# Four transformer mixers, a hybrid block and PEER on one Trainium2 core: another tile order and modulation schedule in GLA, statistics inside the turning at layer ends, FoX values copied by ScalarE

## The chip, the cores and the metric

The kernel runs on one core of one Trainium2 chip. The metric is the device time of one execution in microseconds (us). TensorE (PE) multiplies, VectorE (DVE), ScalarE (ACT) and GpSimd (POOL) work on elements, and SyncE (SP) issues most of the transfers from HBM. Each engine runs its own instructions in the order in which they were written; semaphores join them.

## The reference, cut to what matters

All is float32, for one sequence of 256 tokens and width 1024.

```
cond = silu(c)
for i in range(4):
    mod = cond @ w_mod[i] + b_mod[i]
    shift, scale, gate = split(mod, 3)
    h = rms_norm(x, norm_pre_g[i]) * (1.0 + scale) + shift
    # i = 0, 3: gated linear attention; 1: spatial gating; 2: forgetting attention
    o = (gla_mixer, sgu_mixer, fox_mixer)[i % 3](h, ...)
    x = x + gate * rms_norm(o, norm_post_g[i])
x = x + hybrid_mixer(rms_norm(x, norm_mix), ...)
x = x + peer_ffn(rms_norm(x, norm_ffn), ...)
return rms_norm(x, final_norm)

def gla_mixer(h, ...):
    q, k, v, z, a_low = split(h @ w_in)
    log_a = log_sigmoid(a_low @ w_a2 + b_a) / 16
    # by chunks of 64 tokens: scores q k^T with decay, values, a running state
    o = rms_norm(o, g_head)
    return (o * silu(z)) @ w_out

def fox_mixer(h, ...):
    q, k, v, z, f_logit = split(h @ w_in)
    q, k = rms_norm(q, g_q), rms_norm(k, g_k)
    F = cumsum(log_sigmoid(f_logit + b_f))
    # causal softmax attention with F[q] - F[k] added to the scores
    return (o * silu(z)) @ w_out
```

## The kernel before, in words

**Stages.** After a start of some 37 us come the four mixers one behind the other: GLA (layer 0) to about 170 us, SGU (layer 1) to 292, FoX (layer 2) to 472, GLA again (layer 3) to 599. Then the hybrid block runs to about 925 and PEER to the end. The change touches the four mixers and the place where one layer's output becomes the next layer's input.

**Weights.** A weight tile is 512 KB in HBM (`wr`, 128x1024). SP loads it into one of `RAW = 4` buffers. `w_split` turns it into a high and a low part: ACT writes `wh` (L200), and DVE writes `wl = wr - wh` (L201). A product then takes three matmuls: L403 to L405 in `proj_fm` and L420 to L422 in `proj_tm`. The splits run `LEAD = 5` tiles ahead of the matmuls, in `HIGH = 6` buffers. `proj_fm` ("FM") gives columns by tokens, 24 matmuls of 256 columns for a tile. `proj_tm` ("TM") gives tokens by columns for the two blocks of 128 tokens (tb0 and tb1), matmuls of 512 columns. Projections write into `PJ = 3` PSUM buffers `pj`; other products go to `pm`.

**Ticks.** The functions that work beside the projections are generators. `tick()` is called after each weight tile and lets every listed generator write its next part. The order of the instructions is therefore fixed by how often a generator yields; there is no scheduler.

**Modulation.** For each layer SCALE, SHIFT and GATE are sums over 8 chunks of `w_mod`, 512 KB each. `m_step` does one chunk: DVE multiplies it and adds it to `macc` (L252 for the first of eight, L254 for the others), and SP is given the load of the chunk two further on, in 3 buffers. After the eighth, `m_cols` adds the rows up on PE (L266), copies them on ACT (`rows_copy`, L304), turns them to columns on PE (`rows_to_cols`, L313) and finishes them on DVE as `modc` (L271 to L276), with yields between. GLA layer 0 has 24 steps on its list: GATE of its own, then SCALE and SHIFT of the next layer. `out_proj` turns the GATE columns on PE (L478) and multiplies each output block by them (L484).

**GLA.** Its projections come in the order v (2 TM groups), k (4 FM tiles), q (4), z (8), then the output projection. DVE copies q out of PSUM (L628, `qk`); the scores are L652 and L654, the masks L656.

**Layer ends.** In the last group of `out_proj` all tiles of tb0 come before those of tb1. `late(tb)` makes the statistics of a token block (L355, L492 to L500, one power on POOL), adds to x (L505), norms (L361) and hands over to `make_h`: PE turns two halves of four 128x128 blocks (L367), ACT scales them, DVE writes `hH` and `hL` (L388, L389) in four pairs. The next layer's first projection takes tb0 for a whole tile group and then tb1. The table `FILL` sets when weight splits are written around this place.

**FoX.** q and k leave PSUM on ACT (L830, and squares L832); DVE sums the squares (L833, L840), ACT takes the root (L841, L842), DVE multiplies (L847), and PE turns the result (L790). v is copied by DVE (L861). The forget gate F itself is made elsewhere (L822 and on).

Of the kernel before, what the change touches and what calls it, by code (L numbers as in the profile page):

```python
# [8 lines left out]
F32 = mybir.dt.float32  # L9
F32R = mybir.dt.float32r  # L10
I32 = mybir.dt.int32
U32 = mybir.dt.uint32
AF = mybir.ActivationFunctionType
# [3 lines left out]
P = 128  # L17
# [8 lines left out]
RAW = 4  # L26
HIGH = 6
LEAD = 5
FILL = ((5, 6, 0, 0), (7, 8, 0, 0))
PJ = 3  # L30
RAW2 = 3
HIGH2 = 3
# [29 lines left out]
def _build(ctx, nc, tc, I, out, dbg):  # L62
# [32 lines left out]
    def add(gen, to=tasks):  # L95
        to.append(gen)
# [50 lines left out]
    def plan_fm(t, n, nk=KT):  # L147
        plan.extend((t[c], nk) for c in range(n))
# [4 lines left out]
    for l in range(4):  # L153
        if l in (0, 3):
            j = l // 3
            plan_tm(I["gla_v"][j], 2)
            plan_fm(I["gla_qk"][j], 8)
            plan_fm(I["gla_z"][j], 8)
            plan_tm(I["gla_out"][j], 2)
        elif l == 1:  # L160
            plan_tm(I["sgu_v"], 2)
            plan_fm(I["sgu_uz"], 16)
            plan_tm(I["sgu_out"], 2)
        else:
            plan_tm(I["fox_qkv"], 6)
            plan_fm(I["fox_z"], 8)
            plan_tm(I["fox_out"], 2)
# [38 lines left out]
    def w_fill(n):  # L206
        while nxt_s[0] < n:
            nxt_s[0] += 1
            w_split(nxt_s[0] - 1)
# [48 lines left out]
    def m_cols(l, part):  # L258
        acc = mods.pop((l, part, "acc"))
        mc = tiny.tile([P, 8], F32, tag=f"modc{part}", name="modc", bufs=2)  # L260
        mods[l, part] = mc
        for _ in range(2 if part == SHIFT else 4):
            yield
        p = pm()
        for g in range(4):
            mm(p[32 * g:32 * g + 32, 0:S], ones[:, 0:32], acc[:, g * S:(g + 1) * S], start=True, stop=True)  # L266
        yield
        R = rows_copy(p, 4)
        yield
        pcv = rows_to_cols(p, 4, R)  # L270
        tt(mc.rearrange("p (g t) -> p t g", t=2), pcv.rearrange("p t (g r) -> p t g r", r=32)[:, :, :, 0],  # L271
           col("b_mod", l * 24 + part * 8, 8).rearrange("p (g t) -> p t g", t=2), op=ALU.add)
        if part == SCALE:
            stt(mc, mc, 1.0, col("g_pre", l * 8, 8), op0=ALU.add, op1=ALU.mult)
        elif part == GATE:
            tt(mc, mc, col("g_post", l * 8, 8), op=ALU.mult)  # L276
# [53 lines left out]
    def advance():  # L330

        for g in list(pend):
            if next(g):
                pend.remove(g)
                turning.append(g)

    def settle():
        while pend:
            advance()
        while turning:  # L340
            for _ in turning.pop(0):
                pass
# [27 lines left out]
    def make_h(tb, r, A, B, hs):  # L370

        h, hH, hL = hs
        tsl = slice(tb * P, (tb + 1) * P)
        xn = scaled(tb, r)
        yield True
        ps = [turned(v) for v in xn]
        for m, p in enumerate(ps):
            k4 = slice(4 * m, 4 * m + 4)
            t = h[:, k4, tsl] if h is not None else work.tile([P, 4, P], F32, tag="tl", name="tl", bufs=2)
            for j in range(4):  # L380
                kt = 4 * m + j
                if B is None:
                    act(t[:, j], p[:, j], AF.Copy, scale=A[:, kt:kt + 1])
                else:
                    act(t[:, j], p[:, j], AF.Identity, scale=A[:, kt:kt + 1], bias=B[:, kt:kt + 1])
                if j % 2:
                    e = slice(kt - 1, kt + 1)
                    nc.vector.tensor_copy(hH[:, e, tsl], t[:, j - 1:j + 1])  # L388
                    tt(hL[:, e, tsl], t[:, j - 1:j + 1], hH[:, e, tsl].bitcast(F32), op=ALU.subtract)  # L389

    def proj_fm(n, H, L, consume, nk=KT, per_block=False):

# [19 lines left out]
    def proj_tm(n, H, L, consume, early=False, late=None):  # L412


        def part(p, w, c, tb):
            wh, wl = w
            tsl = slice(tb * P, (tb + 1) * P)
            for k in range(2):
                kt = c * 2 + k
                mm(p, H[:, kt, tsl], wh[:, k], start=(kt == 0), stop=False)  # L420
                mm(p, H[:, kt, tsl], wl[:, k], start=False, stop=False)  # L421
                mm(p, L[:, kt, tsl], wh[:, k], start=False, stop=(kt == KT - 1))  # L422

        for gi in range(n):
            if early and gi == 0 or late is not None and gi == n - 1:
                first = nxt_w[0]
                ws = []
                p = pj()
                for c in range(4):
                    ws.append(w_next(False))  # L430
                    part(p, ws[c], c, 0)
                    advance()
                    if FILL[0][c]:
                        w_fill(first + FILL[0][c])
                consume(gi, 0, p)
                settle()
                if late is not None:
                    pend.append(late(0))
                    advance()
                p = pj()  # L440
                for c in range(4):
                    part(p, ws[c], c, 1)
                    advance()
                    if FILL[1][c]:
                        w_fill(first + FILL[1][c])
                    tick()
                consume(gi, 1, p)
                if late is not None:
                    settle()
                    pend.append(late(1))  # L450
                    advance()
                continue
            ps = [pj() for _ in range(NTB)]
            for c in range(4):
                w = w_next()
                for tb in range(NTB):
                    part(ps[tb], w, c, tb)
                if c == 3:
                    for tb in range(NTB):
                        consume(gi, tb, ps[tb])  # L460
                tick()
# [59 lines left out]
        yield  # L521
        tt(dst, dst, t1, op=ALU.subtract)

    def gated(o, oH, oL, hH, hL, zt, ready, tanh=False):

        zs = {}

        def gate():
            last = None
            for b in range(KT):  # L530
                while b >= ready[0] or b not in zs:
                    yield
                tt(o[:, b], o[:, b], zs.pop(b), op=ALU.mult)
                act(oH[:, b], o[:, b], AF.Copy)
                if last is not None:
                    tt(oL[:, last], o[:, last], oH[:, last].bitcast(F32), op=ALU.subtract)
                last = b
                if b % 2:
                    yield
            tt(oL[:, last], o[:, last], oH[:, last].bitcast(F32), op=ALU.subtract)  # L540

        def c_z(b, p):
            z = zt[:, b]
            if tanh:
                act(z, p, AF.Tanh, scale=0.5)
                stt(z, z, 1.0, p, op0=ALU.add, op1=ALU.mult)
            else:
                act(z, p, AF.Silu)
            zs[b] = z

        add(gate())
        proj_fm(8, hH, hL, c_z, per_block=True)


    def gla(l, hs, lp, nA, nB, nF):
# [58 lines left out]
            have["decay"] = True  # L614

        add(decay())
        add(mod_steps([1] * (8 if l else 24)), later)

        def c_v(g, tb, p):
            if tb == 1:  # L620
# [79 lines left out]
                    yield  # L700

        proj_fm(4, hH, hL, c_k)
        add(mix(0))
        add(mix(1))
        assert have["decay"]
        proj_fm(4, hH, hL, c_q)
        oH = lp.tile([P, KT, S], F32R, tag="kk", name="oH")
        oL = lp.tile([P, KT, S], F32R, tag="qk", name="oL")
        gated(o, oH, oL, hH, hL, lp.tile([P, KT, S], F32, name="zt"), ready)
        drain()  # L710
        return out_proj(oH, oL, lp, ("ls1", "v"), l, nA, nB, nF)

# [91 lines left out]
    def fox(l, hs, lp, nA, nB, nF):  # L804
# [33 lines left out]
        def normed(half):  # L838
            sv = ss[:, half]
            ts(sv, sv, 1.0 / Dh, EPS, op0=ALU.mult, op1=ALU.add)  # L840
            act(sv, sv, AF.Ln)  # L841
            act(sv, sv, AF.Exp, scale=-0.5)  # L842
            yield
            yield
            for tb in range(NTB):
                vw = qk[:, tb, half * D:(half + 1) * D].rearrange("p (h d) -> p h d", d=Dh)
                tt(vw, vw, sv[:, tb, :, None].to_broadcast([P, 16, Dh]), op=ALU.mult)  # L847
                yield
            yield
            yield from transpose_blocks(qk[:, :, half * D:(half + 1) * D], qkT[:, 8 * half:8 * half + 8], 8,  # L850
                                        col("g_k" if half else "g_q"), done)

        add(mod_steps([1] * 24), later)
        add(forget())
        proj_tm(2, hH, hL, c_qk, early=True)
        add(normed(0))
# [1 line left out]
        add(normed(1))  # L858

        def c_v(g, tb, p):  # L860
            nc.vector.tensor_copy(v[:, tb, g * 512:(g + 1) * 512], p)  # L861

        SP = ((0, 0, P), (P, P, S))
        ready = [0]
# [795 lines left out]
```

## Time and profile before

| | |
|---|---|
| median of 3 runs | 1792.31 us (1790.88 to 1793.3) |
| the profiled execution | 1794.16 us |
| its span, first to last instruction | 1792.2 us |
| mean granted TensorE clock | 0.978 of full speed |
| PE busy | 1690.8 us |
| DVE busy | 1286.6 us |
| ACT busy | 970.5 us |

The span is 1.96 us shorter than the time of the same execution. The profiled execution is 1.85 us above the median. PE's busy time holds matmuls at either level of its clock, so a stretch in which PE is always busy can still be slow.

### The profile page before, as it was taken

What the parts mean: (1) busy time and instruction counts of PE and PEld (TensorE: products, weight loads), DVE (VectorE), ACT (ScalarE), POOL (GpSimd) and SP (SyncE); (2) the same over time, 40 slices, a digit from 0 to 9 for tenths busy, and PEclk for the clock granted to TensorE, in tenths of its full rate; (3) what the DMA queues carried; (4) which work ended last, traced back from release to release, by engine and by line L of the source; (5) the groups of instructions that cost most, each with busy time, mean ns of one, the idle gap of its engine ahead of it and who ended that gap; (6) DMA issues with size and microseconds to landing.
All of it is one profiled execution on the core that took longest, in us unless ns stands there. A gap on an engine that the chain in (4) does not pass through costs nothing.

```text
span 1792.2 us, 28529 instructions
## 1 busy us (share of the span) xinstructions
PE 1690.8 (94%) x10774; PEld 1492.5 (83%) x10774; DVE 1286.6 (72%) x2593; ACT 970.5 (54%) x1527; POOL 62.2 (3%) x102
## 2 busy tenths in 40 slices
PE   3979899999989999999999999999999999999997
PEld 2877786767789788888979999998999888888886
DVE  7878787877785856675576889997774466666665
ACT  3436446545644644435454446667995555555554
POOL 0000000000000000000000000000000000000000
PEclk9989999999989999999999999999999999999999
DMA  8765885862463566335654676664557677877775
GB/s 328 262 220 194 285 285 175 302 233 74 146 213 105 158 209 181 118 102 152 187 174 136 206 225 190 204 192 159 150 150 231 214 240 235 234 236 234 236 235 159
DMA packets 104188, 357.08 MB, mean 199 GB/s; under 512 B 12273, under 2 KB 13297, under 8 KB 103794
## 3 DMA queue, kind: packets, MB, share of 16 engines
q1 hardware_dynamic: 97200, 335.52, 59.6%
q0 software_dynamic: 5120, 16.78, 2.4%
q10 hardware_dynamic: 1730, 2.96, 0.5%
q8 instruction: 85, 1.39, 0.3%
q14 instruction: 53, 0.43, 0.1%
HBM read 337.38 MB, written 17.83 MB: 198 GB/s over the span
## 4 chain that ended last, share of the span: by engine, by line
PE 76%; DVE 11%; DMA 5%; ACT 4%; issue 3%; SPq 0%; POOL 0%; DVEq 0%; POOLq 0%; ACTq 0%
PE pm L1447 20%; PE pj L1424 6%; PE pj L1422 6%; PE pj L1423 6%; PE pj L420 5%; PE pj L422 4%; PE pj L421 4%; PE pj L403 4%; DMA wmod<-in_w_mod 4%; PE pj L404 4%; PE pj L405 4%; DVE wl L201 4%; PE pm L1329 3%; DVE macc L254 2%; ACT wh L200 1%
## 5 line engine op out<-in xcount | busy, mean ns | idle before, releaser
L201 DVE TENSOR_TENSOR wl<-wr,wh 128x1024 fp32r<-128x1024 f32 x504 | 614.7, 1224 | 306.0 <-ACT wh L200 305.5
L200 ACT ACTIVATE wh<-wr 128x1024 fp32r<-128x1024 f32 x504 | 528.1, 1055 | 217.9 <-PE pm L1447 54.8
L1422 PE MATMUL pj<-uH,wh 128*128 128x256 f32 x1024 | 293.7, 287 | 0.0
L1424 PE MATMUL pj<-uL,wh 128*128 128x256 f32 x1024 | 289.9, 283 | 0.0
L1423 PE MATMUL pj<-uH,wl 128*128 128x256 f32 x1024 | 289.8, 283 | 0.0
L403 PE MATMUL pj<-hH,wh 128*128 128x256 f32 x768 | 228.1, 297 | 1.6 <-DVE v L623 0.9
L404 PE MATMUL pj<-hH,wl 128*128 128x256 f32 x768 | 222.9, 290 | 0.6 <-DVE wl L201 0.4
L405 PE MATMUL pj<-hL,wh 128*128 128x256 f32 x768 | 222.2, 289 | 0.0
L1447 PE MATMUL pm<-wh 128*128 128x512 f32 x512 | 203.1, 397 | 4.1 <-ACT wh L321 4.1
L1447 PE MATMUL pm<-wl,wh 128*128 128x512 f32 x512 | 202.8, 396 | 0.0
L1447 PE MATMUL pm<-wh,wl 128*128 128x512 f32 x512 | 202.7, 396 | 0.0
L1422 PEld LDWEIGHTS pj<-uH,wh 128*128 128x128 f32 x1024 | 196.7, 192 | 0.0
L1423 PEld LDWEIGHTS pj<-uH,wl 128*128 128x128 f32 x1024 | 196.4, 192 | 0.1
L1424 PEld LDWEIGHTS pj<-uL,wh 128*128 128x128 f32 x1024 | 196.2, 192 | 0.0
L420 PE MATMUL pj<-wh,hH 128*128 128x512 f32 x352 | 146.5, 416 | 22.4 <-DVE hH L388 14.8
L403 PEld LDWEIGHTS pj<-hH,wh 128*128 128x128 f32 x768 | 152.7, 199 | 13.0 <-issue 7.9
L404 PEld LDWEIGHTS pj<-hH,wl 128*128 128x128 f32 x768 | 152.8, 199 | 1.4 <-DVE wl L201 1.3
L405 PEld LDWEIGHTS pj<-hL,wh 128*128 128x128 f32 x768 | 152.6, 199 | 0.0
L422 PE MATMUL pj<-wh,hL 128*128 128x512 f32 x352 | 142.2, 404 | 0.3 <-DVE hL L1527 0.3
L421 PE MATMUL pj<-wl,hH 128*128 128x512 f32 x352 | 141.7, 403 | 0.0
L254 DVE SCALAR_TENSOR_TENSOR macc<-wmod,sc,macc 128x1024 f32<-128x1024 f32 x76 | 97.3, 1281 | 33.3 <-DMA wmod<-in_w_mod 33.0
L1447 PEld LDWEIGHTS pm<-wh 128*128 128x128 f32 x512 | 96.5, 188 | 27.6 <-ACT wh L321 4.3
(337 smaller groups left out, 2679.1 us busy)
## 6 DMA issues: line engine op xcount, KB each, us to landing
wr<-in_down SPq DMA_DIRECT2D x128, 512.0 KB, 3.8
wr<-in_up SPq DMA_DIRECT2D x128, 512.0 KB, 4.3
wmod<-in_w_mod SPq DMA_DIRECT2D x88, 512.0 KB, 5.7
wr<-in_hyb_fm SPq DMA_DIRECT2D x40, 512.0 KB, 3.6
wr<-in_hyb_qkv SPq DMA_DIRECT2D x36, 512.0 KB, 4.3
spill<-st POOLq DMA_DIRECT2D x64, 256.0 KB, 3.8
a<-spill SPq DMA_DIRECT2D x64, 256.0 KB, 3.4
wr<-in_fox_qkv SPq DMA_DIRECT2D x24, 512.0 KB, 4.1
```

Of the source, the lines that this page charges most:

```text
L200: act(wh, w, AF.Copy)
L201: tt(wl, w, wh.bitcast(F32), op=ALU.subtract)
L403: mm(o, wh[:, kt, cs], H[:, kt], start=(kt == 0), stop=False)
L404: mm(o, wl[:, kt, cs], H[:, kt], start=False, stop=False)
L405: mm(o, wh[:, kt, cs], L[:, kt], start=False, stop=(kt == nk - 1))
L420: mm(p, H[:, kt, tsl], wh[:, k], start=(kt == 0), stop=False)
L421: mm(p, H[:, kt, tsl], wl[:, k], start=False, stop=False)
L422: mm(p, L[:, kt, tsl], wh[:, k], start=False, stop=(kt == KT - 1))
L1422: mm(o, wh[:, kt], uH[:, kt], start=(kt == 0), stop=False)
L1423: mm(o, wl[:, kt], uH[:, kt], start=False, stop=False)
L1424: mm(o, wh[:, kt], uL[:, kt], start=False, stop=(kt == KT - 1))
L1447: mm(acc[tb][n], lw[:, m, tsl], ru[:, 0, HALF[n]], start=(i == 0 and lw is wh and ru is uh), stop=(i == P - 1 and lw is wl))
```

## The change: what it does

Five parts. (A) In both GLA layers two of the eight z tiles run between k and q (`ZFIRST = 2`), so that nine FM tiles lie ahead of the first scores and not seven. (B) The modulation steps of GLA layer 0 start eight ticks later and go two to a tick at two places; those of FoX go two in three ticks at first, so that eight of them fall later. (C) `m_cols` waits one more tick between the rows' copy and their turning, for SCALE and GATE. (D) At every layer end the first half of tb0's `hH` and `hL` is written, then tb1's statistics, then the second half; one weight split is written behind that (`LATE_FILL`). (E) FoX's v leaves PSUM by ACT and not by DVE, and the turning of the first normed half (q) is written a tick later.

```diff
+ZFIRST = 2
 FILL = ((5, 6, 0, 0), (7, 8, 0, 0))
+LATE_FILL = ((5, 6, 0, 0), (7, 0, 0, 0))
...
         R = rows_copy(p, 4)
-        yield
+        for _ in range(1 if part == SHIFT else 2):
+            yield
         pcv = rows_to_cols(p, 4, R)
...
                     tt(hL[:, e, tsl], t[:, j - 1:j + 1], hH[:, e, tsl].bitcast(F32), op=ALU.subtract)
+            if m == 0:
+                yield
...
                 consume(gi, 1, p)
                 if late is not None:
-                    settle()
+                    while pend:
+                        advance()
+                    turn = turning.pop()
+                    next(turn)
                     pend.append(late(1))
                     advance()
+                    for _ in turn:
+                        pass
+                    w_fill(first + 8)
...
+        if first:
+            proj_fm(first, hH, hL, c_z, per_block=True)
+            between()
+            oH, oL = oH(), oL()
         add(gate())
-        proj_fm(8, hH, hL, c_z, per_block=True)
+        proj_fm(8 - first, hH, hL, lambda b, p: c_z(first + b, p), per_block=True)
...
-        add(mod_steps([1] * (8 if l else 24)), later)
+        add(mod_steps([1] * 8 if l else [0] * 8 + [1] * 8 + [2] * 4 + [1] * 4 + [2] * 2), later)
...
-            yield
+            for _ in range(1 if half else 2):
+                yield
             yield from transpose_blocks(qk[:, :, half * D:(half + 1) * D], qkT[:, 8 * half:8 * half + 8], 8,
...
-        add(mod_steps([1] * 24), later)
+        add(mod_steps([1, 1, 0] * 8 + [1] * 8), later)
...
-            nc.vector.tensor_copy(v[:, tb, g * 512:(g + 1) * 512], p)
+            act(v[:, tb, g * 512:(g + 1) * 512], p, AF.Copy)
```

DVE's list while PE runs the v tiles of GLA layer 0, before (`wl` are weight splits, `macc` modulation steps, `la` the decay's logarithms):

```order
L201 TENSOR_TENSOR wl<-wr,wh 128x1024
L252 TENSOR_SCALAR macc<-wmod,sc 128x1024
L201 TENSOR_TENSOR wl<-wr,wh 128x1024
L254 SCALAR_TENSOR_TENSOR macc<-wmod,sc,macc 128x1024 x3
L201 TENSOR_TENSOR wl<-wr,wh 128x1024 x2
L518 TENSOR_SCALAR la<-pm,cols 128x256 x4
L254 SCALAR_TENSOR_TENSOR macc<-wmod,sc,macc 128x1024
```

The same place on DVE after the change (the split is now L204, the decay L532):

```order
L642 COPY v<-pj 128x512
L204 TENSOR_TENSOR wl<-wr,wh 128x1024 x4
L532 TENSOR_SCALAR la<-pm,cols 128x256 x4
L204 TENSOR_TENSOR wl<-wr,wh 128x1024 x2
L536 TENSOR_TENSOR la<-la,ls_425 128x1024
```

The eight GATE steps have left this place; they now stand one to a tick from the first k tile on.

DVE's list at the GATE columns of layer 0, before, where they stand right behind the first masks (`A`):

```order
L656 TENSOR_TENSOR A<-pm,tri 128x384 x2
L254 SCALAR_TENSOR_TENSOR macc<-wmod,sc,macc 128x1024
L271 TENSOR_TENSOR modc<-pm,cols 128x2x4
L276 TENSOR_TENSOR modc<-modc,cols 128x8
L201 TENSOR_TENSOR wl<-wr,wh 128x1024
```

After the change (L257 is the modulation step, L275 and L280 the columns) they stand behind the last z tile's gating (`o`, `oL`), with the doubled steps of the output projection behind them:

```order
L257 SCALAR_TENSOR_TENSOR macc<-wmod,sc,macc 128x1024
L204 TENSOR_TENSOR wl<-wr,wh 128x1024
L715 SCALAR_TENSOR_TENSOR o<-o,cols,pm 128x256 x2
L547 TENSOR_TENSOR o<-o,zt 128x256
L550 TENSOR_TENSOR oL<-o,oH 128x256
L547 TENSOR_TENSOR o<-o,zt 128x256
L550 TENSOR_TENSOR oL<-o,oH 128x256
L257 SCALAR_TENSOR_TENSOR macc<-wmod,sc,macc 128x1024
L275 TENSOR_TENSOR modc<-pm,cols 128x2x4
L280 TENSOR_TENSOR modc<-modc,cols 128x8
L554 TENSOR_TENSOR oL<-o,oH 128x256
L257 SCALAR_TENSOR_TENSOR macc<-wmod,sc,macc 128x1024 x2
```

Between the first q copy and these columns there are now 13 modulation steps and 8 splits.

DVE's list at the end of layer 0, before, from tb0's norm (`xn`) to tb1's statistics (`v`, `jk`):

```order
L361 TENSOR_SCALAR xn<-x,rr 128x512 x2
L201 TENSOR_TENSOR wl<-wr,wh 128x1024 x2
L484 TENSOR_TENSOR t_1264<-pj,gate 128x512
L388 CAST hH<-tl 128x2x128
L389 TENSOR_TENSOR hL<-tl,hH 128x2x128
L388 CAST hH<-tl 128x2x128
L389 TENSOR_TENSOR hL<-tl,hH 128x2x128
L388 CAST hH<-tl 128x2x128
L389 TENSOR_TENSOR hL<-tl,hH 128x2x128
L388 CAST hH<-tl 128x2x128
L389 TENSOR_TENSOR hL<-tl,hH 128x2x128
L355 TENSOR_SCALAR v<-ss 128x1
```

The same place on DVE after the change:

```order
L365 TENSOR_SCALAR xn<-x,rr 128x512 x2
L204 TENSOR_TENSOR wl<-wr,wh 128x1024
L275 TENSOR_TENSOR modc<-pm,cols 128x2x4
L498 TENSOR_TENSOR t_1251<-pj,gate 128x512
L392 CAST hH<-tl 128x2x128
L393 TENSOR_TENSOR hL<-tl,hH 128x2x128
L392 CAST hH<-tl 128x2x128
L393 TENSOR_TENSOR hL<-tl,hH 128x2x128
L359 TENSOR_SCALAR v<-ss 128x1
L506 SCALAR_TENSOR_TENSOR jk,ss<-t_1251,x 128x512
L512 TENSOR_TENSOR c<-ss 128x2
L513 SCALAR_TENSOR_TENSOR c<-c,rr 128x1
```

One split has moved from ahead of `hH` to behind its second half, and the statistics stand between the halves; SHIFT's columns have come to stand here too.

## Rows read from the trace of the kernel before

**Rows 1.** The page's first part: busy us, share of the span, instructions.

```profile
PE 1690.8 (94%) x10774; PEld 1492.5 (83%) x10774; DVE 1286.6 (72%) x2593; ACT 970.5 (54%) x1527; POOL 62.2 (3%) x102
```

**Rows 2.** Windows: length, busy us of each engine (instructions), PEclk, DMA share, GB/s.

```profile
0.00:927.00 927.00, 846.37 (x5232) 723.80 (x5232) 663.39 (x1142) 451.47 (x764) 25.56 (x35) 0.96 0.59 195
```

**Rows 3.** Waits of PE from 37 to 927 us: total, times, longest.

```profile
PE pm L652 <- DVE qk L628: 16.1, 2, 10.2
PE pj L420 <- DVE hH L388: 12.6, 8, 1.9
...
PE pj L420 <- DVE v L861: 3.8, 1, 3.8
PE pm L313 <- ACT rows L304: 2.9, 2, 2.0
PE pj L420 <- ACT sq L832: 2.8, 2, 2.4
```

**Rows 4.** Timeline of DVE, GLA layer 0.

```profile
58.36 1.28 DVE L254 SCALAR_TENSOR_TENSOR macc<-wmod,sc,macc 128x1024 f32<-128x1024 f32 x1 [4.80 <-DMA wmod<-in_w_mod]
60.88 1.28 DVE L254 SCALAR_TENSOR_TENSOR macc<-wmod,sc,macc 128x1024 f32<-128x1024 f32 x1 [1.23 <-DMA wmod<-in_w_mod]
62.08 2.35 DVE L201 TENSOR_TENSOR wl<-wr,wh 128x1024 fp32r<-128x1024 f32 x2
...
97.98 0.69 DVE L628 SCALAR_TENSOR_TENSOR qk<-pj,eq 128x512 f32<-128x512 f32 x1
```

**Rows 5.** Timeline of PE, GLA layer 0: first scores, and turning of the GATE columns.

```profile
98.82 1.09 PE L652 MATMUL pm<-qk,kk 128*128 128x64 f32 x4 [10.22 <-DVE qk L628]
...
148.53 0.27 PE L478 MATMUL pm<-ident,modc 128*128 128x128 f32 x1
```

**Rows 6.** Windows of the GLA layers and of FoX's projections, columns as in Rows 2.

```profile
62.08:97.98 35.90, 25.56 (x194) 23.70 (x193) 35.83 (x44) 15.50 (x19) 0.00 (x0) 0.90 0.81 275
65.98:77.50 11.52, 11.52 (x97) 11.46 (x95) 11.45 (x13) 3.42 (x4) 0.00 (x0) 1.00 0.85 282
98.82:108.83 10.01, 10.01 (x50) 10.01 (x51) 5.87 (x8) 0.00 (x0) 0.00 (x0) 0.54 0.72 228
114.96:120.97 6.01, 6.01 (x52) 5.81 (x50) 3.47 (x5) 1.76 (x5) 0.00 (x0) 1.00 0.52 177
98.82:146.00 47.18, 45.87 (x330) 42.91 (x331) 33.99 (x55) 18.79 (x34) 2.13 (x2) 0.90 0.61 204
330.00:372.00 42.00, 35.80 (x161) 27.98 (x160) 37.98 (x41) 19.52 (x29) 0.00 (x0) 0.94 0.94 335
531.72:541.80 10.08, 10.08 (x49) 10.08 (x50) 3.48 (x6) 1.03 (x1) 0.00 (x0) 0.52 0.52 160
```

**Rows 7.** Timeline of ACT and of DVE, FoX's projections.

```profile
336.04 0.23 ACT L841 ACTIVATE ss<-ss 128x32 f32<-128x32 f32 x1 [7.32 <-DVE ss L840]
...
369.97 1.28 DVE L861 COPY v<-pj 128x512 f32<-128x512 f32 x2
```

**Rows 8.** Waits of DVE from 380 to 448 us, FoX's z tiles.

```profile
DVE wl L201 <- ACT wh L200: 16.3, 9, 2.4
```

**Rows 9.** Windows at the ends of layers 0 and 1, columns as in Rows 2.

```profile
172.90:178.70 5.80, 5.78 (x24) 4.35 (x24) 5.39 (x17) 3.30 (x7) 1.92 (x2) 1.00 0.43 153
181.50:192.20 10.70, 10.61 (x39) 8.51 (x40) 7.95 (x13) 6.01 (x10) 0.00 (x0) 0.84 0.83 279
295.05:302.40 7.35, 7.35 (x26) 5.82 (x27) 6.94 (x19) 3.29 (x7) 1.85 (x2) 0.77 0.42 157
305.00:310.60 5.60, 5.60 (x27) 3.19 (x26) 5.21 (x11) 3.41 (x6) 0.00 (x0) 1.00 0.46 138
```

**Rows 10.** Timeline of DVE, end of layer 0: tb1's statistics, its x, its first `hH`.

```profile
175.22 0.21 DVE L355 TENSOR_SCALAR v<-ss 128x1 f32<-128x1 f32 x1
...
176.86 1.41 DVE L505 SCALAR_TENSOR_TENSOR x<-t,rr,x 128x512 f32<-128x512 f32 x2
...
181.25 0.29 DVE L388 CAST hH<-tl 128x256 fp32r<-128x256 f32 x1
```

More of the change, by code (lines that the diff above doesn't have):

```diff
@@ L156, in _build @@
             plan_tm(I["gla_v"][j], 2)
-            plan_fm(I["gla_qk"][j], 8)
-            plan_fm(I["gla_z"][j], 8)
+            qk, z = I["gla_qk"][j], I["gla_z"][j]
+            plan.extend((t[c], KT) for t, c0, c1 in ((qk, 0, 4), (z, 0, ZFIRST), (qk, 4, 8), (z, ZFIRST, 8))
+                        for c in range(c0, c1))
             plan_tm(I["gla_out"][j], 2)
@@ L426, in proj_tm @@
                 first = nxt_w[0]
+                last = late is not None and gi == n - 1
+                fill = LATE_FILL if last else FILL
                 ws = []
@@ L432, in proj_tm @@
                     advance()
-                    if FILL[0][c]:
-                        w_fill(first + FILL[0][c])
+                    if fill[0][c]:
+                        w_fill(first + fill[0][c])
                 consume(gi, 0, p)
@@ L443, in proj_tm @@
                     advance()
-                    if FILL[1][c]:
-                        w_fill(first + FILL[1][c])
+                    if fill[1][c]:
+                        w_fill(first + fill[1][c])
                     tick()
@@ L522, in log_sigmoid, with gated @@
         tt(dst, dst, t1, op=ALU.subtract)
-    def gated(o, oH, oL, hH, hL, zt, ready, tanh=False):
+    def gated(o, oH, oL, hH, hL, zt, ready, tanh=False, first=0, between=None):
         zs = {}
@@ L549, in c_z @@
             zs[b] = z
+        if first:
+            proj_fm(first, hH, hL, c_z, per_block=True)
+            between()
+            oH, oL = oH(), oL()
         add(gate())
-        proj_fm(8, hH, hL, c_z, per_block=True)
+        proj_fm(8 - first, hH, hL, lambda b, p: c_z(first + b, p), per_block=True)
+        return oH, oL
     def gla(l, hs, lp, nA, nB, nF):
@@ L702, in gla, with queries @@
         proj_fm(4, hH, hL, c_k)
[L703 to L709, printed above, removed]
+        def queries():
+            add(mix(0))
+            add(mix(1))
+            assert have["decay"]
+            proj_fm(4, hH, hL, c_q)
+        oH, oL = gated(o, lambda: lp.tile([P, KT, S], F32R, tag="kk", name="oH"),
+                       lambda: lp.tile([P, KT, S], F32R, tag="qk", name="oL"), hH, hL,
+                       lp.tile([P, KT, S], F32, name="zt"), ready, first=ZFIRST, between=queries)
         drain()
```

## The prediction

> **What bounds the kernel now.** I first read how busy the engines are. PE works 1690.8 us, 94% of the span [rows 1], so time is won or lost where PE stands still or runs at the lower clock. The change touches the first 927 us. There PE is busy for 846.4 us and stands for 80.6, at a mean clock of 0.96 [rows 2]. Next I read PE's waits in that stretch [rows 3]. Five groups stand where the change works. The scores of the two GLA layers wait 16.1 us for q's copy on DVE, 10.2 in one and therefore 5.9 in the other. The first projection at layer ends waits 12.6 us in eight parts for `hH`. One projection in FoX waits 3.8 us for the v copy and another most of 2.8 for ACT's squares. The modulation rows cost 2.9, of which 2.0 in one place, SGU. Last I asked for windows, since a busy PE tells nothing of its clock.
>
> **GLA layer 0.** From 62.08 to 97.98 DVE is busy 35.83 of 35.90 us, while PE has work for 25.6 [rows 6]. So q's copy, at 97.98, is late because DVE's list is long. Ahead of it DVE also stood 4.8 and 1.2 us for `w_mod` transfers [rows 4]. From start to start a modulation step takes 60.88 to 62.08, 1.2 us, and a split 2.35/2 = 1.18 [rows 4]. Part B takes eight steps (8 x 1.2 = 9.6) from ahead of the copy. Part A puts two more z tiles ahead of it, each with a step and a split (2 x 2.38 = 4.8). The copy then starts at 97.98 - 9.6 + 4.8 = 93.2 and ends at 93.9. I count nothing for the two waits on transfers, since without steps DVE can run ahead there only as far as there are split buffers. PE has four FM tiles in 11.52 us, 2.88 each [rows 6]; nine tiles from 65.98 end at 91.9. The wait of 10.2 becomes 2.0, and the scores start at 93.9, not 98.82: 4.9 us.
>
> The clock comes with it. From 98.82 to 108.83 PE is busy throughout with 50 matmuls at a clock of 0.54. The second half, 52 matmuls of the same kinds, takes 6.01 at 1.00 [rows 6]: 4.0 us lost after the stall. With a stall of 2 us I leave 1.0 of it and count 3.0. The two z tiles are missing later (5.8), and the later of the two `rows` waits (2.9 - 2.0 = 0.9) goes. PE would turn the GATE columns at 148.53 [rows 5] - 4.9 - 3.0 - 5.8 - 0.9 = 133.9, 14.6 earlier.
>
> But those columns come later now, since GATE's steps were moved. Between the end of the first q copy and the columns DVE has 13 steps (15.6) and 8 splits (9.4). The rest of its work in that stretch I take from 98.82 to 146: 34.0 busy [rows 6] less nine steps and nine splits (21.4) is 12.6. Idle time there is 47.2 - 34.0 = 13.2; less 4 further doubled steps that fit into it (4.8) and less the 4.0 of slow clock, 4.4 stay. The columns come at 93.9 + 15.6 + 9.4 + 12.6 + 4.4 = 135.9, 2.0 after PE: a **new stall**. I count 14.6 - 2.0, less another 2.5 for a low clock behind the new stall and for doubled loads (the DMA share was 0.81 while one step fell to a tick [rows 6]): **-10**. Bounds: without the stall -14.6; if the whole 13.2 of idle time stays (8.8 more), -4.
>
> **SGU, part C.** The wait of 2.0 us for rows [rows 3] is taken up by one more tile of 2.88: **-2**. For GLA layer 0 the extra tick is in the list above; elsewhere a tick hides it, as no consumer stands near.
>
> **FoX, parts B and E.** From 330 to 372 DMA is 0.94 busy and DVE 38.0 of 42 us [rows 6]. ACT waits 7.3 us for DVE's last sums at 336.04, and PE then waits behind ACT. At 369.97 DVE copies two v blocks (1.28) out of PSUM behind its queue, and PE waits 3.8 for the buffer [rows 7, 3]. ACT is busy only 19.5 of 42 there [rows 6], so v on ACT leaves as PE ends it, and one step in three less shortens DVE's queue and the load on DMA. I take away 2.4 + 3.8, and the low clock of this window, 42 x 0.06 = 2.5 [rows 6], less 0.7 for a remnant: **-8** (bounds -9 and -3, if only the v wait goes). The eight steps that fall later (9.6) meet z tiles in which DVE waits 16.3 us for ACT's splits [rows 8], and cost nothing. Without that cover they would cost up to 9.6.
>
> **GLA layer 3, part A alone.** The two tiles ahead give PE 5.8 us more work and DVE two splits, 2.4. The wait of 5.9 becomes 2.5: 3.4 gained. From 531.72 to 541.80 PE runs 49 matmuls at 0.52, 4.1 us above the 6.01 [rows 6]; half of it stays. **-5.5** (bounds -2.4 and -10).
>
> **Five layer ends, part D.** DVE is the bound here. From tb1's statistics at 175.22 to tb1's `hH` at 181.25 it has no gap [rows 10], and before that the four pairs. The part reorders that work and moves one split behind, but tb1's `hH` stands behind the same sum: not earlier. tb0 can start a split earlier, about 1 us, at 172 instead of 173. PE then finishes tb0 earlier and waits longer for tb1. What changes is the clock. Layer 0's end has tb0 at 1.00 (24 matmuls in 5.80) and pays behind tb1's gap: 10.70 us at 0.84, a loss of 10.7 x 0.16 = 1.7. Layer 1's end has tb0 at 0.77 (7.35) and tb1 at 1.00 (27 matmuls in 5.60) [rows 9]; the slow tb0 costs nothing there, as DVE is later still. With one short and one long gap I expect the loss to move to tb1 at the ends of layers 1, 2 and 3, whose `hH` waits are of one kind in the eight of [rows 3]: 3 x 1.7, less 1 for what the early start gives: **+4** (bounds -5, 1 us gained at each of five, and +8.5, all five pay).
>
> Here the Trainium skill speaks against the change: "TensorE: Matmul & The Clock Gate", section "Part 4: PE-mode transpose", says that transposes do not count as PE work for the clock. By it the transposes would not break up the longer gap and all five ends would pay, +8.5 instead of +4, a total of 1775. The trace is mixed: it shows tb0 behind the transposes at 1.00 at one end and 0.77 at the next.
>
> **Sum.** -10 - 2 - 8 - 5.5 + 4 = -21.5. The durations are from an execution of 1794.16 us (span 1792.2 and 1.96 around it), 1.85 above the median; I put the difference on the median: 1792.31 - 21.5 = **1771** us.
>
> **Rivals.** (1) GATE's columns decide layer 0: the 13.2 us of idle time stay, since loads of 512 KB now come two to a tick and DVE waits for them in order, as at 58.36 [rows 4]. Then layer 0 gives -4, in all -15.5: 1777. Against it: those steps have three buffers and no v tiles beside them. (2) The layer ends gain, 1 us each, and no clock is lost: -30.5, 1762. For it: tb1's clock was 1.00 at layer 1's end. (3) The changes of FoX and GLA layer 3 only move the wait to the next copy on DVE (bounds -3 and -2.4): -13.4, 1779. For it: DVE stays the fuller engine there. (4) Slower: the halves at the layer ends. The second half of `hH` now stands behind the statistics (175.22 to 176.86, 1.6 us [rows 10]), and x behind the second half. If tb0 waits those 1.6 in its middle, runs at half clock (7.35 - 5.60 = 1.75), tb1 starts 1.6 later and pays 1.7, that is 6.65 at each of five ends, 33 us against -25.5: 1800. It decides from 5.1 us an end on. Against it: the second half is needed only after 12 matmuls of tb0, and those last 2.9 us. (5) The change does not do what it says: steps moved in ticks come to stand behind the same copies and only order changes, within 0.2%. Against it: eight steps have left the v tiles in DVE's list.
>
> **How the numbers follow.** Chances: forecast 0.55 (its own range 1765 to 1776), (1) 0.15, (2) 0.12, (3) 0.09, (4) 0.04, (5) 0.05. The range from 1758 to 1781 takes in (1), (2) and (3), and the ends of the layer bounds that fall together only now and then. About 0.2%, 3.6 us, is what a measurement of this kernel tells from no change. Faster by more than that: 0.91; within it 0.05; slower 0.04.
>
> **What would show it.** Right, if the first scores of layer 0 start near 94 after a wait of 2 us at most and the next window is near full clock; if a new wait of PE stands before the GATE turning; if ACT's v copy leaves no wait in FoX; if SGU's wait for rows is gone. At the layer ends tb0 should start 1 us after its transposes and tb1 at the same distance from the layer's end as now, with a lower clock. The prediction is wrong if DVE's wait for `w_mod` grows in layer 0's q and z tiles, if FoX's eight steps lengthen its z tiles, or if tb1's start moves by more than a microsecond.

## The result and the profile after

The changed kernel takes 1773.01 us in the median of four runs (1771.11 to 1774.21), the kernel before 1791.6 in the same series. The ratio is 0.9891 with a 95% interval from 0.9878 to 0.9904: faster, by 17 to 22 us. In a later series the same kernel gave 0.9883 (0.9866 to 0.9899). The forecast was 1771 and 21.5 us.

The first part of the page after, with the engines' busy time:

```profile
PE 1682.3 (95%) x10774; PEld 1485.2 (84%) x10774; DVE 1284.5 (73%) x2589; ACT 973.6 (55%) x1531; POOL 60.6 (3%) x102
```

The span is 1770.6 and not 1792.2 us. PE's busy time fell by 8.5 us with the same number of instructions, so some of the gain is clock; the other 13 us are idle time that is gone. PE's waits from 37 to 927 us, after (total, times, longest):

```profile
PE pj L426 <- DVE hH L392: 14.6, 10, 2.4
...
PE pm L492 <- DVE modc L280: 3.6, 1, 3.6
PE pj L410 <- DVE wl L204: 3.2, 3, 1.8
PE pm L671 <- DVE qk L647: 2.5, 1, 2.5
...
PE pm L317 <- ACT rows L308: 0.7, 1, 0.7
```

Beside [rows 3]: the scores' 16.1 us became 2.5. The v copy and the squares in FoX are off the list, and the rows' wait of 2.0 is gone. New are 3.6 us ahead of the turning of the GATE columns (L492) and 3.2 us for weight splits. The ten waits for `hH` can't be set against the eight of [rows 3] as they stand: the end of the hybrid block now comes within the 927 us, and 2.2 of the 14.6 us are its two. At the four ends of the layers the waits are 12.6 us before and 12.4 after; tb0's became shorter (7.7 to 4.1) and tb1's longer (4.9 to 8.3).

To see where the time went I cut each execution at PE's first turning (L367, after the change L371) at each of the five layer ends: 169.95, 292.10, 472.45, 599.45 and 924.77 us before, 165.58, 286.74, 459.07, 577.90 and 904.74 after. The differences are the lengths of the stages; each begins with the layer end ahead of it.

| stage, us | before | after | after, second profile |
|---|---|---|---|
| start and GLA layer 0 | 169.9 | 165.6 | 166.2 |
| SGU | 122.2 | 121.2 | 118.7 |
| FoX | 180.3 | 172.3 | 169.8 |
| GLA layer 3 | 127.0 | 118.8 | 119.6 |
| hybrid | 325.3 | 326.8 | 324.1 |
| PEER | 867.4 | 865.9 | 867.0 |
| span | 1792.2 | 1770.6 | 1765.5 |

The last column is the same program in another series, below. Three stages differ by 2.5 to 2.8 us between the two. A stage of one execution must therefore not be read closer than that. What makes the difference in FoX and in the hybrid block is shown with the layer ends. Layer 0's own program is the same in five of the profiled executions (the changed kernel twice and the three with FoX's old parts), and in these it ends between 164.7 and 166.9 us.

### The profile page after: what moved, and what is told of

The parts are those of the page before. It is cut to its first block, busy times and chain, and to the rows that moved or that the text cites. A ratio compares the mean times of both kernels' runs of the same rounds, so it can differ in the third digit from the quotient of the medians.

```text
span 1770.6 us, 28535 instructions
## 1 busy us (share of the span) xinstructions
PE 1682.3 (95%) x10774; PEld 1485.2 (84%) x10774; DVE 1284.5 (73%) x2589; ACT 973.6 (55%) x1531; POOL 60.6 (3%) x102
## 4 chain that ended last, share of the span: by engine, by line
PE 78%; DVE 12%; ACT 3%; DMA 3%; issue 3%; POOL 0%; SPq 0%; DVEq 0%; POOLq 0%; ACTq 0%
PE pm L1470 20%; PE pj L1447 6%; PE pj L1445 6%; PE pj L1446 6%; PE pj L426 5%; PE pj L428 5%; PE pj L427 5%; DVE wl L204 4%; PE pj L409 4%; PE pj L410 4%; PE pj L411 4%; PE pm L1352 3%; DMA wmod<-in_w_mod 2%; DVE macc L257 2%; ACT wh L203 1%
## 5 line engine op out<-in xcount | busy, mean ns | idle before, releaser
L204 DVE TENSOR_TENSOR wl<-wr,wh 128x1024 fp32r<-128x1024 f32 x504 | 614.3, 1223 | 308.0 <-ACT wh L203 307.1
L426 PE MATMUL pj<-wh,hH 128*128 128x512 f32 x352 | 144.9, 412 | 15.5 <-DVE hH L392 14.6
L1470 PEld LDWEIGHTS pm<-wh,wl 128*128 128x128 f32 x512 | 96.8, 189 | 22.7 <-DVE wl L326 0.2
```

What stands on the lines that cost most here:

```text
L204: tt(wl, w, wh.bitcast(F32), op=ALU.subtract)
L1470: mm(acc[tb][n], lw[:, m, tsl], ru[:, 0, HALF[n]], start=(i == 0 and lw is wh and ru is uh), stop=(i == P - 1 and lw is wl))
```

## The experiments

All ratios are to the kernel before. The kernels of one series ran on one chip and share the runs of the kernel before.

| kernel | median, us | ratio | 95% interval |
|---|---|---|---|
| changed | 1773.01 | 0.9891 | 0.9878 to 0.9904 |
| first series: without part D | 1769.08 | 0.9880 | 0.9858 to 0.9902 |
| two splits behind tb1's hH | 1774.26 | 0.9891 | 0.9872 to 0.9910 |
| GATE columns of layer 0 a tick earlier | 1771.28 | 0.9880 | 0.9862 to 0.9899 |
| layer 0's steps as before | 1770.85 | 0.9877 | 0.9859 to 0.9896 |
| second series: ZFIRST = 0 | 1781.72 | 0.9936 | 0.9924 to 0.9949 |
| FoX's steps as before | 1773.74 | 0.9898 | 0.9879 to 0.9917 |
| v by DVE | 1774.62 | 0.9897 | 0.9879 to 0.9914 |
| without part C | 1775.66 | 0.9902 | 0.9886 to 0.9917 |
| third series: both FoX parts as before | 1780.05 | 0.9928 | 0.9914 to 0.9941 |
| kernel before, with part D alone | 1793.65 | 1.0011 | 1.0001 to 1.0020 |
| without D and layer 0's extra ticks | 1771.60 | 0.9884 | 0.9869 to 0.9899 |
| changed, once more | 1770.38 | 0.9883 | 0.9866 to 0.9899 |

### Layer 0: steps as before, and GATE a tick earlier

```diff
-        add(mod_steps([1] * 8 if l else [0] * 8 + [1] * 8 + [2] * 4 + [1] * 4 + [2] * 2), later)
+        add(mod_steps([1] * 8 if l else [1] * 24), later)
```

> The changed kernel with the modulation steps of layer 0 one to a tick from the first v tile on, as before; the two z tiles stay ahead of the scores. Theory: q's copy comes 9.6 us of steps later, at about 103, against nine tiles of PE that end at 92, so the first scores wait some 10 us again, while the wait for the GATE columns goes: layer 0 loses its gain of 4 us, 1777, ratio 0.992. Rival: layer 0 is bound by DVE's sum over its whole length and the place of the steps does not matter: 1773, ratio 0.989.

Measured 0.9877, no slower than the changed kernel: the theory failed, the rival held. PE's waits from 37 to 927 us in that kernel:

```profile
PE pm L671 <- DVE qk L647: 7.2, 1, 7.2
```

The scores wait 7.2 us, as the theory said in kind, and the wait for the GATE columns is gone. But layer 0 ends at 165.25, against 165.58 with the new steps. What is lost at the scores is not lost behind them. The windows from the first scores to the layer's end, first with the new steps (kernel after the change), then with the old (length, busy us of each engine, PEclk, DMA share, GB/s):

```profile
94.15:165.58 71.43, 66.15 (x402) 56.87 (x403) 57.19 (x90) 29.78 (x55) 4.08 (x4) 0.90 0.71 241
101.83:165.25 63.42, 63.13 (x392) 55.60 (x393) 46.73 (x82) 28.81 (x53) 4.07 (x4) 0.93 0.58 200
```

With the old steps the scores start 7.7 us later. Behind them PE then stands for 0.3 us and not for 5.3, and the low clock takes 4.4 us (63.42 x 0.07) and not 7.1 (71.43 x 0.10). The two together give the 7.7 back.

```diff
-        for _ in range(1 if part == SHIFT else 2):
+        for _ in range(2 if part == SCALE or part == GATE and l else 1):
```

> The changed kernel with the extra tick of part C taken back for the GATE columns of layer 0 alone. Theory: in layer 0 the columns stand one z tile too far back in DVE's list, and that alone makes PE's new wait of 3.6 us ahead of the GATE turning and the low clock behind it (2.1 us); the columns now come one tick, some 4.4 us, earlier, and the wait goes: 5 us faster than the changed kernel, 1768, ratio 0.9865. Rival: layer 0 ends where DVE's whole list ends, so the wait only moves into the output projection, and the time stays at 1773, ratio 0.989.

Measured 0.9880 (0.9862 to 0.9899): the interval holds the rival's 0.989 and just the theory's 0.9865, so the time does not settle it. The waits of PE from 37 to 927 us:

```profile
PE pm L671 <- DVE qk L647: 3.8, 1, 3.8
...
PE pm L317 <- ACT rows L308: 2.9, 1, 2.9
...
PE pm L269 <- DVE macc L257: 1.4, 1, 1.4
```

The wait at L492 is gone, and two others stand behind it: for the last modulation step (1.4) and for the rows of the next column set (2.9). Layer 0 ends at 167.44 in this execution, no earlier than in the changed kernel. The wait moved, as the rival said. Both runs point to one thing: in layer 0 the place of the steps and of the columns decides where PE waits, and not how long the layer is. That DVE's list alone holds the layer is an argument and not shown: DVE is idle for 14.2 of the 71.4 us behind the scores, and no run made its list shorter there.

### Tile order in the two GLA layers

```diff
-ZFIRST = 2
+ZFIRST = 0
...
+        if not ZFIRST:
+            queries()
         oH, oL = gated(o, ...
```

> The changed kernel with ZFIRST = 0: z behind q in both GLA layers, all else as changed. Theory: in layer 3 the two z tiles cover the wait for q's copy; without them the scores wait 5.9 us again at half clock behind, and layer 3 is 5 to 8 us longer. In layer 0, where steps at their old place and GATE columns a tick earlier left the end of the layer where it was, DVE's sum is the bound, so the order of PE's tiles changes nothing there: layer 0 ends within 1.5 us of 165.6. In all 6 us slower than the changed kernel, 1779, ratio 0.993. Rival: in layer 0 too the tiles are what took the wait away; then its end goes back to about 170 and the whole is 10 us slower, 1783, ratio 0.995.

Measured 0.9936, which is apart from the changed kernel by both intervals: part A is worth some 8 to 9 us (1781.72 against 1773.01, or the ratio's difference of 0.0045). The scores of the two layers wait 9.2 us together again:

```profile
PE pm L672 <- DVE qk L648: 9.2, 2, 5.6
```

Layer 3 takes 125.3 us, 6 more than with the order of the change (118.8 and 119.6), as the theory said. Layer 0 ends at 168.5, between theory and rival: 2.3 to 2.9 us of its gain are the order's, by one execution.

### FoX: either part, and neither

```diff
-        add(mod_steps([1, 1, 0] * 8 + [1] * 8), later)
+        add(mod_steps([1] * 24), later)
```

> The changed kernel with FoX's modulation steps one to a tick, as before. Theory: the fuller DVE list and the fuller transfers of FoX's first 24 tiles make q's norm late, so PE's wait behind ACT's squares comes back with some low clock: 3 to 4 us slower than the changed kernel, 1776, ratio 0.991. Rival: v on ACT alone took both waits away, since it frees PSUM buffers and DVE time; no change, 1773, ratio 0.989.

```diff
-            act(v[:, tb, g * 512:(g + 1) * 512], p, AF.Copy)
+            nc.vector.tensor_copy(v[:, tb, g * 512:(g + 1) * 512], p)
```

> The changed kernel with FoX's v copied by DVE, as before. Theory: the copy stands behind steps, splits and norms on DVE, PE waits for the PSUM buffer some 3 us and runs at half clock for 2 to 3 behind it: 5 us slower than the changed kernel, 1778, ratio 0.992. Rival: with one step in three taken out DVE's list is short enough, the copy comes in time, no change: 1773, ratio 0.989.

Measured 0.9898 and 0.9897: both rivals hold within the intervals. The second theory's 0.992 is out by the time. The first's 0.991 is within its interval, but PE's wait behind ACT's squares, on which it rested, is not in that trace. FoX takes 172.6 and 172.9 us, against 172.3 and 169.8. Then both at once:

> The changed kernel with both of FoX's old parts: v copied by DVE and steps one to a tick; the later turning of q stays. Each alone left FoX at 172.6 to 172.9 us between its two layer ends, as in the changed kernel, against 180.4 in the kernel before. Theory: the two parts take the same waits away and either is enough; with both undone PE waits again some 3 us for the v copy, and behind ACT's squares, with low clock: FoX at 179 to 181, in all 1780, ratio 0.993. Rival: FoX's gain came from neither (but from the tick of part C or from the later turning of q): FoX stays at 173 and the whole at 1773, ratio 0.989.

Measured 0.9928, 1780.05 us, as the theory said. FoX takes 180.1, as before the change. PE's waits from 290 to 475 us in this kernel:

```profile
PE pj L426 <- DVE v L884: 5.4, 1, 5.4
...
PE pj L426 <- ACT sq L854: 1.3, 1, 1.3
```

The 5.4 us for the v copy are the old wait of 3.8, now longer: it ends 78.4 us behind the layer's first turning (at 364.59), before the change 78.6 (at 370.71). So the two parts are worth 7 to 10 us together (1780.05 against 1773.01 and 1770.38), and either is enough: fewer steps bring the copy in time, and a copy on ACT doesn't need them fewer.

### Without the extra tick

```diff
-        for _ in range(1 if part == SHIFT else 2):
+        for _ in range(1):
             yield
```

> The changed kernel without part C anywhere. Theory: SGU's wait for the copied rows (2.0 us) comes back and nothing else, since a GATE tick in layer 0 alone made no difference: 2 us slower than the changed kernel, 1775, ratio 0.990. Rival: the splits that PE waits for in SGU's first FM tiles set its pace and take the wait in, no change: 1773, ratio 0.989.

Measured 0.9902, 1775.66, with an interval that holds the changed kernel too: not settled by the time. The trace shows both sides. In SGU PE waits again, from 182 to 284 us:

```profile
PE pm L317 <- ACT rows L308: 1.7, 1, 1.7
```

SGU takes 122.6 us, but layer 0 ends at 161.5, the earliest of all. The tick takes that wait away in SGU. That it costs in layer 0 is not shown. The window from the first scores to the end of layer 0 in this execution:

```profile
94.25:161.49 67.24, 62.19 (x403) 53.42 (x403) 56.56 (x90) 29.08 (x54) 4.08 (x4) 0.97 0.75 251
```

PE stands for 5.1 us, as with the tick (5.3). What is different is the clock, 0.97 and not 0.90, or 2.0 us lost (67.24 x 0.03) and not 7.1. The run below that leaves out the tick for layer 0's GATE and the next SCALE alone ends layer 0 at 164.4.

### Layer ends

Without part D, and with FILL in both places:

```diff
-            if m == 0:
-                yield
...
-                    while pend:
-                        advance()
-                    turn = turning.pop()
-                    next(turn)
+                    settle()
                     pend.append(late(1))
                     advance()
-                    for _ in turn:
-                        pass
-                    w_fill(first + 8)
```

> The changed kernel without part D: tb0's four pairs of hH and hL in one piece, tb1's statistics behind them, the splits of FILL as before. Theory: part D costs, since tb1's start is set by DVE's sum, which D does not shorten, and the longer second gap moves the low clock from tb0's matmuls (free) to tb1's (paid). Then this kernel is faster than the changed one by 5 us: 1768, ratio to the kernel before 0.9865; its windows at the ends of layers 1 and 2 show tb0's 24 matmuls in 7.35 us and tb1's at full clock. Rival: the earlier start of tb0 is worth 1 us at each end, then this kernel is slower, 1777, ratio 0.992.

Measured 0.9880 (0.9858 to 0.9902): the interval holds both the changed kernel and the theory's 0.9865, and leaves out the rival's 0.992. The windows at the end of layer 1 (tb0, then tb1) are as the theory said:

```profile
286.88:294.05 7.17, 7.17 (x25) 5.66 (x26) 6.75 (x18) 3.30 (x7) 1.86 (x2) 0.76 0.47 158
296.41:302.41 6.00, 6.00 (x27) 3.49 (x28) 5.62 (x11) 3.80 (x7) 0.00 (x0) 1.00 0.55 165
```

Part D put on the kernel before, the same lines with the other sign:

> The kernel before with part D alone. Theory: D costs what taking it from the changed kernel gave (some 4 us, of it 2.7 in FoX): tb1's start stays within 0.6 us after each first transposing, tb0 ends early, and tb1's first matmuls run at half clock at the ends of layers 1, 2 and 3: 1796, ratio 1.002. Rival: without the other parts the shorter wait of tb0 counts, 1 us at each end: 1789, ratio 0.998.

Measured 1.0011 (1.0001 to 1.0020), the only run of D by itself: by the interval, which just leaves out 1, it costs 0.2 to 3.6 us. The rival's 0.998 is out. The window from tb1's start at the end of layer 1 in that kernel:

```profile
305.46:311.46 6.00, 6.00 (x19) 3.95 (x20) 4.44 (x10) 2.29 (x3) 0.00 (x0) 0.72 0.47 147
```

19 matmuls at 0.72 stand where [rows 9] had 27 in 5.60 us at 1.00: the low clock did move from tb0 (now 1.00 from 295.02 to 301.02) to tb1. It did so at the end of layer 2 too (0.72), and not at the end of layer 3 (1.00), where the theory had it as well.

Then the splits behind tb1's `hH`:

```diff
+EARLY_FILL = ((0, 0, 0, 0), (7, 8, 0, 0))
...
-                fill = LATE_FILL if last else FILL
+                fill = LATE_FILL if last else EARLY_FILL
```

> The changed kernel with the two weight splits that stand between tb1's norm and tb1's hH on DVE moved behind tb1's hH. Theory: DVE's list alone sets tb1's start, so tb1 starts 2.35 us earlier at four layer ends, and with the shorter gap the low clock (1.5 us an end) goes at some of them: 9 to 15 us faster than the changed kernel, 1758 to 1764, ratio 0.982 to 0.985. Rival: tb1's start is set by PE's transposes and ACT's scaling behind them; then tb1 starts at most 0.5 us earlier and the later splits make PE wait in the next tiles: 1772 to 1776, ratio 0.989 to 0.992.

Measured 0.9891, no difference, as the rival said of the time. tb1 started 0.9, 1.6, 1.6 and 1.1 us earlier after its layer's first turning, so neither the 2.35 of the theory nor the 0.5 of the rival is right: the two splits are part of what tb1 waits for; what holds the rest no run sets apart. PE's wait for tb1 is 0.7 to 0.8 us here, the granted clock behind it is 1.00 at all four ends, FoX took 169.7 us and hybrid 324.6. But the other layers lost it again: SGU took 122.7 us and layer 3 121.9, and layer 0 ended at 167.8. In SGU the later splits are missing in the tiles that follow, in layer 3 PE waits 3.1 us for a copy of v on DVE, a wait that neither execution of the changed kernel has. PE's waits from 37 to 200 us, with that of SGU's first FM tile (at 199.63):

```profile
PE pj L411 <- DVE wl L205: 4.2, 1, 4.2
```

Two corrections together, and the changed kernel again:

```diff
-        for _ in range(1 if part == SHIFT else 2):
+        for _ in range(1 if part == SHIFT or (l, part) in ((0, GATE), (1, SCALE)) else 2):
```

(and part D undone as above)

> The changed kernel without part D, and without part C's extra tick for the two column sets of layer 0 (its GATE and the next layer's SCALE); SGU and FoX keep the tick. Theory: the two corrections add: 4 us from the layer ends and 4 us in layer 0, which ends at some 161.5 as in the kernel without the tick, while SGU keeps its gain: 8 us faster than the changed kernel, 1765, ratio 0.9845. Rival: the end of layer 0 is given back in SGU, where splits set the pace: 1769, ratio 0.9865.

> The changed kernel once more, on the chip of the three others, so that differences of 0.2% can be read against it. All theories: 1773, ratio 0.989; its stage lengths show how far executions of one program differ.

Measured 0.9884 and 0.9883. Neither the theory's 0.9845 nor the rival's 0.9865 came. The corrections do not add to anything that shows; layer 0 ended at 164.4, not 161.5, with 3.8 us of waits for rows. No kernel of this study is clearly faster than the changed one.

## Why the prediction was right

The total was right to 2 us (1771 against 1773.01), and so were the signs of the five terms. Single terms were off and cancelled: layer 0 gave 6 us less than forecast, layer 3 gave 2 to 3 more and FoX up to 2.5 more. So the closeness of the total is partly luck.

**GLA layer 0, forecast -10, measured -4.4 and -3.7: too large.** The first half was right. PE's timeline at the first scores and at the GATE columns, after:

```profile
94.15 0.41 PE L671 MATMUL pm<-qk,kk 128*128 128x64 f32 x2 [2.50 <-DVE qk L647]
...
140.52 1.09 PE L492 MATMUL pm<-ident,modc 128*128 128x128 f32 x4 [3.56 <-DVE modc L280]
```

The scores were forecast for 93.9 after 2.0 us and came at 94.15 after 2.50. The sign that the next window is near full clock did not come (0.69, below). The new stall was forecast, but 2.0 and not 3.56 us, with the columns at 135.9 and not 140.4. The step that failed is the idle time of DVE between q's copy and the columns. Two windows after, of the slow stretch and of DVE's stretch from the copy to the columns (length, busy us of each engine, PEclk, DMA share, GB/s):

```profile
94.15:105.00 10.85, 10.85 (x61) 10.69 (x62) 7.22 (x8) 0.94 (x3) 0.00 (x0) 0.69 0.94 345
94.00:140.40 46.40, 41.82 (x298) 38.05 (x298) 37.62 (x60) 18.12 (x34) 2.13 (x2) 0.91 0.77 265
```

DVE is busy 37.6 us, just the 15.6 + 9.4 + 12.6 of the forecast. It is idle 8.8, where I had left 4.4 of 13.2. I had let the four doubled steps fill 4.8 of that idle time and had let the slow clock go (4.0). The clock did not go: 10.85 us at 0.69 lose 3.4 (10.85 x 0.31), where I had counted 1.0. So a stall of 2.5 us costs nearly the clock that 10.2 us had cost. The tail behind the columns also cost more: 25.1 us from L492 to the layer's end, 21.4 before (148.53 [rows 5] to 169.95), 3.6 instead of 2.5. Rival (1) gave the right size, -4, with the wrong cause: DVE's wait for `w_mod` transfers in the stretch is one of 0.8 us. DVE waits there for other engines: 4.8 us for ACT's squares (`sq`) and 2.0 for PE's products ahead of the masks (`A`). The run with the old steps fits that: with the steps where they were, layer 0 ends at the same place. What part B does in layer 0 is nothing that shows. Part A's 2 to 3 us are the only gain there that an experiment sets apart; the rest is no more than executions of the same layer differ by (164.7 to 166.9 us).

**GLA layer 3, forecast -5.5, measured -8.2 and -7.4.** The two extra tiles covered the wait wholly; 2.5 us of it should have stayed. Without part A the layer takes 125.3 us in its one execution; with it 118.8 to 122.2 in the eleven that there are, and the two of the changed program lie at the short end. So A's term was nearly right (3 to 6.5 us by these); the other 1 to 2 us are not accounted for by a run.

**FoX, forecast -8, measured -8.0 and -10.5.** The mechanism is right and the size was low. The -8.0 holds some 2.5 us that part D costs at the end of layer 1, which belongs to this stage (below). Without that cost FoX takes 169.7 to 169.9 us, some 10.5 less than the 180.3 before and past the bound of -9. The kernel before with D alone took 177.8 there, so the term is known to 2 or 3 us only. The window of FoX's projections that answers to 330 to 372 in [rows 6]:

```profile
324.00:366.00 42.00, 42.00 (x204) 34.09 (x204) 35.49 (x37) 23.71 (x35) 0.00 (x0) 1.00 0.89 309
```

PE is busy throughout at full clock, with 204 matmuls instead of 161. What I had not seen is that B and E are each enough alone; as a sum of two parts the term would have been counted twice. That the eight steps which fall later cost nothing also held: with the old steps FoX was as long.

**SGU, forecast -2, measured -1.0 and -3.5.** The wait for rows is gone, and comes back with 1.7 us without part C. Splits in the first FM tiles took some of it (3.2 us in three waits in the first execution, 2.0 in the second).

**Layer ends, forecast +4 at five.** The mechanism is right. tb0 starts 2.03 us behind its first turning at the end of layer 1 (286.74 to 288.77) and not 2.95; tb1 starts 12.47 behind it (299.21) and not 12.50 (304.60). At the other three ends tb1's start moves by 0.1 to 0.6 us, within the microsecond that the prediction allowed. The price is +2 us by the ratio of the kernel before with D alone (1.0011), and no more than 3.6. The count of five was wrong: the end of the hybrid block runs as before (`hH` waits of 1.56 and 0.66 us on both sides), so there are four, and the eight waits of [rows 3] were already the two of four ends. Nor is the price paid in every execution. The end of layer 1 in the two executions of the changed program, first the timeline of PE at tb1's first matmul:

```profile
299.21 0.64 PE L426 MATMUL pj<-wh,hH 128*128 128x512 f32 x1 [2.36 <-DVE hH L392]
```

and the window around it:

```profile
298.00:304.00 6.00, 4.79 (x14) 3.44 (x15) 4.36 (x11) 2.57 (x6) 0.00 (x0) 0.72 0.53 175
```

In the other execution the timeline of PE has:

```profile
297.40 0.50 PE L426 MATMUL pj<-wh,hH 128*128 128x512 f32 x1 [2.37 <-DVE hH L392]
```

and the window:

```profile
296.20:302.20 6.00, 4.80 (x21) 2.99 (x22) 5.47 (x13) 3.49 (x6) 0.00 (x0) 1.00 0.55 175
```

The waits ahead are 2.36 and 2.37 us and the work is the same; the granted clock is 0.72 in one and 1.00 in the other. That is 1.7 us (6.00 x 0.28) in this window, and FoX is 2.5 us longer in the first.

The other profiled executions show which of the two is the rule. At the end of layer 1 tb1 waits 2.36 or 2.37 us in ten of them, all with part D (the kernel before with D is one). In nine the granted clock over the 6 us from tb1's start is 0.72 and in one, the second shown, 1.00. In the three without D tb1 waits 1.3 us and has 1.00, and tb0 has 0.72. Among the kernels with at least one new part of FoX, FoX takes 172.3 to 173.0 us in the seven with the low clock behind tb1 and 169.7 to 169.9 in the four without (the second profile, the two without D, and the one with the splits behind tb1's `hH`). So D costs some 2.5 to 3 us here in most executions. At the end of layer 3 the clock behind tb1 is 0.72 to 0.74 in three of the nine changed kernels with D and its splits unmoved; the hybrid block takes 326.8 to 327.1 us in these and 323.9 to 324.1 in the other six. That is the hybrid block's difference in the table of stages. At the ends of layers 0 and 2 the low clock comes and goes too, but the stage behind does not follow it: in the table SGU takes 121.2 us with 1.00 there and 118.7 with 0.72. These are single executions of several kernels, grouped afterwards, and not an experiment of their own.

The weighing of the Trainium skill's rule on transposes ("TensorE: Matmul & The Clock Gate", "Part 4: PE-mode transpose") therefore stays open: transposes stand in the gap both times, and the clock falls once.

## What to carry to other kernels

Moving work within one engine's list can move the wait of another engine and leave the stage's end where it was, as with layer 0's modulation steps (165.25 us with the old place, 165.58 with the new). What took a wait away here was other work that was ready for the waiting engine, the two z tiles, or less work in the list, as in FoX. Two remedies against one queue are not two gains: undo each alone, and then both, before adding them up. A stall that is short can cost as much clock as a long one, and whether it does can differ between two executions of one program, so gains of a few microseconds need an interval over several executions and cannot be read from one profile.

## What the hardware showed unexpectedly

One program can take the lower clock in one execution and not in the next. With equal waits of 2.36 and 2.37 us ahead of the same matmuls the clock went to 0.72 of full speed over 6 us in one execution and stayed at 1.00 in the other; at this place nine of ten executions with such a wait had the low clock. The stages of the two executions differ by 2.5 (SGU), 2.5 (FoX) and 2.8 us (hybrid) and by at most 1.2 in the others, in spans of 1770.6 and 1765.5.
